# Attention in three products of float16 halves, with the order of projections, weight splits and turned outputs moved around it

## The chip, the cores and the metric

The kernel runs on one core of a Trainium2 chip. The metric is the time of one execution on the device in microseconds. A run of the program on the chip gives one such time; where a median is given, it is over several runs. A profile is one execution taken by the hardware profiler.

## What is computed

A decoder trunk of two layers on 256 tokens of width 1024, all in float32. Each layer normalises its input, projects it with one matrix into the inputs of four causal token mixers of four heads each (A: forgetting attention with a cumulative log-forget bias; B: sliding window with two key heads and sinks; C: multi-head latent attention with a rotary part; D: dilated windows), joins their outputs, projects them back and adds; then comes a feed-forward block, dense in layer 0, two of eight experts in layer 1. Cut to what matters here:

```python
for layer in range(DEPTH):                       # DEPTH = 2
    h = rms_norm(x, attn_norm[layer])
    (fq, fk, fv, ff, sq, sk, sv, cq, ckv, kr, dq, dk, dv) = jnp.split(h @ w_in[layer], splits, axis=-1)
    y_a, y_b, y_c, y_d = fox_mixer(...), swa_sink_mixer(...), mla_mixer(...), dilated_mixer(...)
    x = x + jnp.concatenate([y_a, y_b, y_c, y_d], axis=-1) @ w_out[layer]
    h = rms_norm(x, ffn_norm[layer])
    x = x + (swiglu(h, ...) if layer % 2 == 0 else moe_swiglu(h, ...))
return rms_norm(x, final_norm)
# in every mixer, a head: s = q @ k.T * scale + bias; p = softmax(s, causal); o = p @ v
```

## The kernel before

**Float16 halves of weights.** Every large weight is loaded as float32 by a DMA of about 1 MB that the SP queue issues (`load_next`, L162) and split on the chip into a high and a low float16 half: ScalarE writes the high one (`high_part`, L169), VectorE the low one, the rest (`low_part`, L172). A product with such a weight is three float16 matmuls (`mm3`, L458 to L461: high by high, high by low, low by high). `Stream` keeps the order: units of weights in the order of their use; `split_next` gives out one unit's high part and the low parts of the units before it; `done` counts a used unit and calls `go`, which splits up to `ahead` units past the used one (`ahead` starts at 3 and grows to 5, one at every second unit from the sixth on). `done` stops short of both while `later` is set.

**Attention in float32.** The projections leave q and k transposed (heads' columns in partitions) and v by tokens, as float32 tiles; `out_T` (L564) writes q and k from PSUM with one VectorE instruction that applies the scale and the norm factor `rb`. For head i of 16 (four each of A, C, D, B), `qk(i)` (L753) makes the scores of two blocks of 128 queries with float32 matmuls over 64 rows (C has a second product over 32 rows for its rotary part, A adds float16 products with a triangle, L774, for the forget bias), then VectorE adds the mask and takes the row extreme (L785) and ScalarE takes the exponential (L790). `tr(i)` (L799) transposes the probabilities on TensorE and copies them to `pT` on ScalarE (L805). `pv(i)` (L811) multiplies them with v in three float32 matmuls of 64 columns (L819); after a group's fourth head VectorE divides into `o` (L827), and `turn_out` (L833) transposes that and leaves the two halves of `mix` (L841, L842) for the output projection `wo_job`.

**Order.** Each engine runs its instructions in the order in which the program gives them out. The loop over i (L845 on) gives out, for each i: the scores of head i, a job of projection or of output projection from the queue `fills`, `pv` of head i - 2, `tr` of head i - 1. The fills are, in order: the two halves of D's q (the second with `mla_b`, which transposes the normalised latents), `mla_c` (the rotary q, q, k and v of C), `mla_d` with D's k, D's v, B's q, k and v, then the output projections of A, C, D. A's v, q and k come before the loop. `turn_out` of A, D and B stands ahead of the job of its turn, that of C behind it.

Of the kernel before, what the change touches and what calls it, by code (L numbers as in the profile page):

```python
# [11 lines left out]
F32 = mybir.dt.float32  # L12
F16 = mybir.dt.float16
# [26 lines left out]
C = 96  # L40
# [29 lines left out]
def hybrid_trunk_kernel(ctx: ExitStack, tc: tile.TileContext, a: dict, out: bass.AP, dbg=None):  # L70
# [56 lines left out]
    for layer in range(DEPTH):  # L127
# [9 lines left out]
        j = layer // 2  # L137
# [360 lines left out]
    def attention(layer, act, feed, follow):  # L498
# [11 lines left out]

        qT, kT, vv = {}, {}, {}

        def alloc(g):
            slot = "A" if g == "B" else g
            if g == "C":
                qT[g], kT[g] = (mid[:, c0 : c0 + 512].rearrange("p (j s) -> p j s", j=2) for c0 in (1024, 1536))
            else:
                qT[g] = act.tile([P, 2, S], F32, tag=f"q{slot}", name=f"q{g}_{layer}")
                kT[g] = act.tile([P, 2, S], F32, tag=f"k{slot}", name=f"k{g}_{layer}")
            vv[g] = act.tile([P, NT, 256], F32, tag=f"v{slot}", name=f"v{g}_{layer}")  # L520

        c_sb = late_t[:, : NT * 416].rearrange("p (t n) -> p t n", t=NT)
        psm = [bank("acc", f"mla{layer}{t}") for t in range(NT)]
# [37 lines left out]
                first_done.pop()()  # L561
            return ps

        def out_T(dst, ps, scale, p=(0, P), q=(0, P)):  # L564
            ve.scalar_tensor_tensor(
                dst[q[0] : q[1]], ps[p[0] : p[1], :S], scale, rb[p[0] : p[1], :], op0=OP.mult, op1=OP.mult
            )

        def job_T(g, d, m, scale):
            out_T(d[g][:, m, :], proj_T(m), scale)  # L570
            if m == 1:
                unit_done()

# [6 lines left out]

        def job_S(g, t, n, c0):
            ps = proj_S(t, n, c0)
            ve.tensor_scalar(vv[g][:, t, :n], ps[:, :n], rs[:, t : t + 1], None, op0=OP.mult)
            if t == 1:
                unit_done()

# [30 lines left out]
        late = {}  # L617

        def mla_b():
            cT = late_t[:, : 3 * S].rearrange("p (j s) -> p j s", j=3)  # L620
            late["cqT"], late["ckT"] = cT[:, 0:2], cT[:, 2]
            rT = late_t[:, 832:1600].rearrange("p (j s) -> p j s", j=3)
            late["qr"] = rT[:, 2].rearrange("p (t h i) -> p t h i", t=NT, h=4)
            late["qrT"], late["krT"] = rT[:, 0], rT[:, 1]
            p1, p2 = bank("acc", f"mt{layer}a"), bank("acc", f"mt{layer}b")
            for j in range(3):
                ps, c0 = (p1, j * S) if j < 2 else (p2, 0)
                for t in range(NT):
                    te.transpose(ps[:, c0 + t * P : c0 + (t + 1) * P], cn[:, t, j * P : (j + 1) * P], ident)
            for t in range(NT):  # L630
                te.transpose(p2[:, S + t * P : S + (t + 1) * P], kr[:, t, :, :].rearrange("p h i -> p (h i)"), ident)
            se.copy(late["cqT"], p1.rearrange("p (j s) -> p j s", j=2))
            ve.tensor_copy(late["ckT"], p2[:, :S])
            ve.tensor_copy(late["krT"], p2[:, S:])

        def mla_c():
            alloc("C")
            cqT, ckT = late["cqT"], late["ckT"]
            ps = bank("acc", f"mr{layer}")
            for t in range(NT):  # L640
                for k in range(2):
                    te.matmul(ps[:, t * P : (t + 1) * P], cqT[:, k, t * P : (t + 1) * P], wqr[:, k, :], start=k == 0, stop=k == 1)
            rope(ve, late["qr"], ps[:, :S].rearrange("p (t h i) -> p t h i", t=NT, h=4), 0, 4, rtmp)
            ps = bank("acc", f"mq{layer}")
            for j in range(2):
                for k in range(2):
                    te.matmul(ps[:, j * S : (j + 1) * S], wqn[:, k, j * P : (j + 1) * P], cqT[:, k, :], start=k == 0, stop=k == 1)
            se.activation(qT["C"], ps.rearrange("p (j s) -> p j s", j=2), AF.Copy, scale=-(96.0**-0.5))
            ps = bank("acc", f"mk{layer}")
            for j in range(2):  # L650
                te.matmul(ps[:, j * S : (j + 1) * S], wkn[:, j * P : (j + 1) * P], ckT, start=True, stop=True)
            se.copy(kT["C"], ps.rearrange("p (j s) -> p j s", j=2))
            ps = bank("acc", f"mv{layer}")
            for t in range(NT):
                te.matmul(ps[:, t * S : (t + 1) * S], ckT[:, t * P : (t + 1) * P], wkv, start=True, stop=True)
            se.copy(vv["C"], ps.rearrange("p (t s) -> p t s", t=NT))

        def mla_d():
            ps = bank("acc", f"mrt{layer}")
            for t in range(NT):  # L660
                te.transpose(ps[:, t * P : (t + 1) * P], late["qr"][:, t, :, :].rearrange("p h i -> p (h i)"), ident)
            se.copy(late["qrT"], ps[:, :S])

        QS = -(HD**-0.5)
        alloc("A")
# [1 line left out]
        for t in range(NT):  # L667
            ps = proj_S(t, 260)
            ve.scalar_tensor_tensor(z[:, t, :], ps[:, 256:260], rs[:, t : t + 1], bf_bc[:, layer, :], op0=OP.mult, op1=OP.add)
            ve.tensor_scalar(vv["A"][:, t, :], ps[:, 0:256], rs[:, t : t + 1], None, op0=OP.mult)  # L670
        unit_done()
        e1 = atile([P, NT, 4], "e1")
        ve.scalar_tensor_tensor(e1, z, -1.0, z, op0=OP.mult, op1=OP.min)
# [6 lines left out]
        ge.tensor_copy(lbh, lfb)  # L680
        ge.tensor_tensor(lbl, lfb, lbh, op=OP.subtract)
        for d, sc_ in ((qT, QS), (kT, 1.0)):
            stream[0].later = layer > 0 and d is qT
            for m in range(2):
                job_T("A", d, m, sc_)
                if m == 0 and d is qT:
                    mla_norm()
# [19 lines left out]
        def skjob():  # L707
            ps = proj_T(0)
            kb = kT["B"]
            out_T(kb[:, 0, :], ps, 1.0)  # L710
            out_T(kb[:, 1, :], ps, 1.0, (64, 128), (0, 64))
            out_T(kb[:, 1, :], ps, 1.0, (0, 64), (64, 128))

        def svjob():
            for t in range(NT):
# [37 lines left out]
        def qk(i):  # L753
# [1 line left out]
            ps = bank("sc", f"sc{layer}_{i}")  # L755
            b0 = 64 * (h % 2)
            m = h // 2
            q = qT[g][b0 : b0 + 64, m, :]
            k = kT[g][b0 : b0 + 64, (h % 2) ^ m if g == "B" else m, :]
            prods = [(q, k)]  # L760
            if g == "C":
                prods.append((late["qrT"][32 * h : 32 * h + 32, :], late["krT"][32 * h : 32 * h + 32, :]))
            for t in range(NT):
                nk = (t + 1) * P
                c0 = t * P
# [33 lines left out]
        def tr(i):  # L799
            tt = live[i]  # L800
            ps = bank("pt", f"tp{layer}_{i}")
            for j in range(3):
                te.transpose(ps[:, j * P : (j + 1) * P], tt[:, j * P : (j + 1) * P], ident)
            pT = act.tile([P, 384], F32, tag="pT", name=f"pT{layer}_{i}", bufs=2)
            se.copy(pT, ps[:, :384])  # L805
            live[i] = pT

        def pv(i):
            g, h = heads[i]
            pT = live.pop(i)  # L810
            if h == 0:  # L811
                live["o"] = bank("o", f"o{layer}_{i}")
            ps = live["o"]
            vh = h // 2 if g == "B" else h
            vc = slice(vh * 64, (vh + 1) * 64)
            for t in range(NT):
                for j in range(t + 1):
                    c0 = (t + j) * P
                    te.matmul(ps[:, t * S + h * 64 : t * S + (h + 1) * 64], pT[:, c0 : c0 + P], vv[g][:, j, vc], start=j == 0, stop=j == t)  # L819
# [23 lines left out]

        NHD = len(heads)
        for i in range(NHD + 3):  # L845
            if i < NHD:
                qk(i)
            if layer == 0 and i == 2:
                nc.sync.dma_start(bias[:, 1:], a["c_bias"][:, 1:])
            if layer == DEPTH - 1 and i in (5, 10, 16):  # L850
                stream[0].load_next({5: "e0", 10: "e2", 16: "e3"}[i])
            if i in (6, 14, 18):
                turn_out({6: "A", 14: "D", 18: "B"}[i])
            if i == NHD + 1 and layer == DEPTH - 1:
                late["gain"] = act.tile([P, 3, 384], F32, tag="tt", name="gain").rearrange("p a s -> p (a s)")[:, :D]
                ge.dma_start(late["gain"], spread(a["ffn_norm"][layer], D))
            if i == NHD:
                if layer < DEPTH - 1:
                    hold(True)
                else:  # L860
                    stream[0].low_until(stream[0].split)
            fills.popleft()()
            if i == 15:
                fills.popleft()()
            if i == 10:
                turn_out("C")
            if 0 <= i - 2 < NHD and i != 17:
                pv(i - 2)
            if 0 <= i - 1 < NHD:
# [533 lines left out]
```

## Time and profile before

| what | us |
|---|---|
| median of three runs (1367.72 to 1370.78) | 1368.82 |
| the profiled execution's own time | 1368.37 |
| its span, first to last instruction | 1366.6 |

The span runs through five stages: the start and A's projections, layer 0's attention, its dense block, layer 1's attention, the experts. [...] A timeline gives an instruction's (or a run of equal ones') start, its time, engine, line, operation, what it writes and reads, shape, count, and in brackets how long the engine had been idle and what ended that. Matmuls overlap their neighbours, so the step from one start to the next tells more than the time shown. A group of the costliest-groups view gives count, busy time, the mean time of one in ns, and the idle time before them.

### The profile page before, as it was taken

The numbers are of one execution on the slowest core, as the hardware profiler recorded it, in microseconds if no ns is written. First come the engines' busy times: TensorE is split into PE (matmuls) and PEld (weight loads), VectorE is DVE, ScalarE is ACT, GpSimd is POOL, SyncE is SP. The second block draws the span as 40 slices with busy tenths as digits, with TensorE's granted clock in tenths as the row PEclk, the third lists the DMA queues.
The fourth block names the chain that finished last, engine by engine and source line by source line (L and its number), as shares of the span: only waits on it lengthen the run. The fifth ranks groups of instructions, "written<-read, shape, count | busy, mean of one in ns | idle before, by whom it ended". The sixth has DMA issues, their size and how long they took to land.

```text
span 1366.6 us, 43224 instructions
## 1 busy us (share of the span) xinstructions
PE 1277.3 (93%) x19680; PEld 1134.5 (83%) x19680; DVE 1079.5 (79%) x1032; ACT 898.2 (66%) x916; POOL 32.4 (2%) x51
## 2 busy tenths in 40 slices
PE   8999999999999998999999998998998998999885
PEld 5785877777587688999989988998998998999874
DVE  6655775666564587899998898898898998989976
ACT  6554654444544576788777678677777776877764
POOL 2300000000010010000000000000000000000000
PEclk9999999999999999999999999999999999999998
DMA  9953475646443459999999999999999999999991
GB/s 272 353 171 124 155 247 198 203 149 203 156 172 111 175 196 392 400 406 414 413 411 416 412 412 416 411 411 412 408 414 402 403 416 408 410 405 407 412 361 57
DMA packets 128799, 434.35 MB, mean 318 GB/s; under 512 B 11936, under 2 KB 59440, under 8 KB 128480
## 3 DMA queue, kind: packets, MB, share of 16 engines
q1 hardware_dynamic: 126640, 429.72, 81.4%
q8 instruction: 156, 2.56, 0.8%
q0 software_dynamic: 928, 1.78, 0.5%
q14 instruction: 35, 0.29, 0.1%
q10 hardware_dynamic: 1040, 0.00, 0.0%
HBM read 430.41 MB, written 1.06 MB: 316 GB/s over the span
## 4 chain that ended last, share of the span: by engine, by line
PE 23%; DMA 19%; DVE 11%; issue 5%; ACT 3%; SPq 0%; DVEq 0%; ACTq 0%
DMA stg<-in_moe_w_down_dram 13%; DVE lo L172 8%; PE my L1190 5%; DMA stg<-in_moe_w_up_dram 3%; DMA stg<-in_moe_w_gate_dram 3%; PE mu L1151 2%; PE my L1192 2%; PE mg L1161 2%; PE mg L1158 2%; PE mg L1157 2%; PE mg L1151 1%; ACT hi L169 1%; PE mu L1158 1%; PE mu L1157 1%; PE mu L1161 1%
## 5 line engine op out<-in xcount | busy, mean ns | idle before, releaser
L172 DVE SCALAR_TENSOR_TENSOR lo<-stg,hi 128x1792 f16<-128x1792 f32 (+3 forms) x418 | 849.4, 2078 | 44.0 <-ACT hi L169 43.8
L169 ACT ACTIVATE hi<-stg 128x1792 f16<-128x1792 f32 (+3 forms) x418 | 714.4, 1738 | 154.0 <-DMA stg<-in_moe_w_down_dram 56.7
L1158 PEld LDWEIGHTS <-hi 128*128 128x128 f16 x3136 | 271.8, 98 | 11.3 <-issue 11.1
L1157 PEld LDWEIGHTS <-hi 128*128 128x128 f16 x3136 | 272.7, 99 | 4.2 <-issue 4.0
L1192 PE MATMUL my<-rest,hi 128*128 128x96 f16 x1792 | 182.9, 208 | 0.9 <-issue 0.9
L1190 PE MATMUL my<-rest,hi 128*128 128x96 f16 x1792 | 183.0, 208 | 0.3 <-issue 0.3
L1190 PEld LDWEIGHTS <-hi 128*128 128x128 f16 x1792 | 157.6, 99 | 6.2 <-issue 3.3
L1192 PEld LDWEIGHTS <-hi 128*128 128x128 f16 x1792 | 157.2, 99 | 4.1 <-issue 1.0
L1157 PE MATMUL mg<-xgh,hi 128*128 128x96 f16 x1568 | 151.3, 208 | 8.0 <-DVE x L1224 6.0
L1158 PE MATMUL mg<-xgl,hi 128*128 128x96 f16 x1568 | 151.5, 208 | 5.4 <-issue 5.3
L1161 PEld LDWEIGHTS <-lo 128*128 128x128 f16 x3136 | 146.3, 98 | 5.2 <-issue 3.5
L1157 PE MATMUL mu<-xgh,hi 128*128 128x96 f16 x1568 | 147.1, 206 | 0.1
L1158 PE MATMUL mu<-xgl,hi 128*128 128x96 f16 x1568 | 147.1, 206 | 0.0
L1190 PE MATMUL my<-rest,lo 128*128 128x96 f16 x1792 | 115.4, 208 | 7.9 <-DVE lo L172 7.2
L1190 PEld LDWEIGHTS <-lo 128*128 128x128 f16 x1792 | 89.6, 99 | 9.6 <-DVE lo L172 8.6
L1161 PE MATMUL mg<-xgh,lo 128*128 128x96 f16 x1568 | 86.7, 207 | 2.9 <-issue 2.9
L1161 PE MATMUL mu<-xgh,lo 128*128 128x96 f16 x1568 | 85.2, 206 | 0.1
L459 PEld LDWEIGHTS <-hi 128*128 128x128 f16 x640 | 62.6, 98 | 9.9 <-issue 2.7
L460 PEld LDWEIGHTS <-hi 128*128 128x128 f16 x640 | 62.6, 98 | 7.2
L461 PEld LDWEIGHTS <-lo 128*128 128x128 f16 x640 | 62.6, 98 | 7.2
L1179 ACT CAST rest<-sg 128x480 f16<-128x480 f32 (+1 forms) x48 | 27.1, 566 | 60.4 <-DVE sg L1178 60.4
L1151 PE MATMUL mu<-xr,stg 128*128 128x96 f32 x448 | 64.4, 312 | 0.0
(355 smaller groups left out, 1868.2 us busy)
## 6 DMA issues: line engine op xcount, KB each, us to landing
stg<-in_moe_w_gate_dram SPq DMA_DIRECT2D x128, 896.0 KB, 17.9
stg<-in_moe_w_up_dram SPq DMA_DIRECT2D x128, 896.0 KB, 17.4
stg<-in_moe_w_down_dram SPq DMA_DIRECT2D x111, 1024.0 KB, 19.2
stg<-in_w_in_dram SPq DMA_DIRECT2D x14, 1024.0 KB, 7.0
stg<-in_dense_w_gate_dram SPq DMA_DIRECT2D x14, 1024.0 KB, 6.5
stg<-in_dense_w_up_dram SPq DMA_DIRECT2D x14, 1024.0 KB, 5.1
stg<-in_dense_w_down_dram SPq DMA_DIRECT2D x14, 1024.0 KB, 5.0
stg<-in_w_out_dram SPq DMA_DIRECT2D x8, 1024.0 KB, 9.0
```

The source lines that it names most:

```text
L169: se.activation(self.high[u][:, c], self.stage[u][:, c], AF.Copy, scale=SW)
L172: ve.scalar_tensor_tensor(lo[:, c], self.stage[u][:, c], SW, self.high[u][:, c], op0=OP.mult, op1=OP.subtract)
L459: te.matmul(ps, lh, rh, start=first, stop=False)
L460: te.matmul(ps, lh, rl, start=False, stop=False)
L461: te.matmul(ps, ll, rh, start=False, stop=last)
L1151: te.matmul(ps[b][:, c * C : (c + 1) * C], w[0][:, j * P : (j + 1) * P], xr, start=False, stop=ends and j + 1 == spans[b][1])
L1157: te.matmul(dst, L, xh[:, k, :], start=k == 0 and c == 0, stop=False)
L1158: te.matmul(dst, L, xl[:, k, :], start=False, stop=False)
L1161: te.matmul(ps[b][:, c * C : (c + 1) * C], lo[:, j * P : (j + 1) * P], xh[:, k, :], start=False, stop=ends and j + 1 == spans[b][1])
L1179: se.copy(hi[:, c], sg[:, c])
L1190: te.matmul(dst, W, L[0], start=first and part == 0 and d % 4 == 0, stop=ends and part == 1 and d % 4 == 3)
L1192: te.matmul(dst, W, L[1], start=False, stop=False)
```

## The change

The q, k, v, the rotary parts and the transposed probabilities are kept as two float16 halves in the room of the float32 tile, and every product of the scores and of the values becomes three float16 products. The halves are made by `part2`: ScalarE copies the high one out of PSUM, VectorE subtracts. `out_T` first scales in place in PSUM, then calls `part2`; the second copy of B's keys, with the two heads' partitions exchanged, is made by two VectorE copies of the halves. Three changes of order go with it: at i = 0 the fill goes ahead of the scores of head 0; `later` is set for A's k in layer 0, for both q and k in layer 1, until the scores of head 1 are given out, and `go` is called there; `turn_out` of A and D goes behind the fill of its turn.

```diff
+        def part2(hi, lo, src, scale=None):
+            if scale is None:
+                se.copy(hi, src)
+                ve.tensor_tensor(lo, src, hi, op=OP.subtract)
+            else:
+                se.activation(hi, src, AF.Copy, scale=scale)
+                ve.scalar_tensor_tensor(lo, src, scale, hi, op0=OP.mult, op1=OP.subtract)
...
-        def out_T(dst, ps, scale, p=(0, P), q=(0, P)):
-            ve.scalar_tensor_tensor(
-                dst[q[0] : q[1]], ps[p[0] : p[1], :S], scale, rb[p[0] : p[1], :], op0=OP.mult, op1=OP.mult
-            )
+        def out_T(dst, ps, scale):
+            ve.scalar_tensor_tensor(ps[:, :S], ps[:, :S], scale, rb, op0=OP.mult, op1=OP.mult)
+            part2(dst[0], dst[1], ps[:, :S])
...
-            ve.tensor_scalar(vv[g][:, t, :n], ps[:, :n], rs[:, t : t + 1], None, op0=OP.mult)
+            part2(vv[g][:, 0, t, :n], vv[g][:, 1, t, :n], ps[:, :n], rs[:, t : t + 1])
...
-            ve.tensor_copy(late["krT"], p2[:, S:])
+            part2(late["krT"][:, 0], late["krT"][:, 1], p2[:, S:])
...
-            se.activation(qT["C"], ps.rearrange("p (j s) -> p j s", j=2), AF.Copy, scale=-(96.0**-0.5))
+            part2(qT["C"][:, 0], qT["C"][:, 1], ps.rearrange("p (j s) -> p j s", j=2), -(96.0**-0.5))
...
-            stream[0].later = layer > 0 and d is qT
+            stream[0].later = layer > 0 or d is kT
...
-            out_T(kb[:, 0, :], ps, 1.0)
-            out_T(kb[:, 1, :], ps, 1.0, (64, 128), (0, 64))
-            out_T(kb[:, 1, :], ps, 1.0, (0, 64), (64, 128))
+            out_T([kb[:, i, 0, :] for i in range(2)], ps, 1.0)
+            ve.tensor_copy(kb[0:64, :, 1, :], kb[64:128, :, 0, :])
+            ve.tensor_copy(kb[64:128, :, 1, :], kb[0:64, :, 0, :])
...
+            prods = [(qq[:, i], kk[:, j]) for qq, kk in pairs for i, j in ((0, 0), (0, 1), (1, 0))]
...
-            pT = act.tile([P, 384], F32, tag="pT", name=f"pT{layer}_{i}", bufs=2)
-            se.copy(pT, ps[:, :384])
+            pT = act.tile([P, 2, 384], F16, tag="pT", name=f"pT{layer}_{i}", bufs=2)
+            part2(pT[:, 0], pT[:, 1], ps[:, :384])
...
+                    mm3(ps[:, t * S + h * 64 : t * S + (h + 1) * 64], L, R, j == 0, j == t)
...
         for i in range(NHD + 3):
+            if i == 0:
+                fills.popleft()()
             if i < NHD:
                 qk(i)
+            if i == 1:
+                stream[0].later = False
+                stream[0].go()
...
-            if i in (6, 14, 18):
-                turn_out({6: "A", 14: "D", 18: "B"}[i])
...
-            fills.popleft()()
+            if i == 18:
+                turn_out("B")
+            if i > 0:
+                fills.popleft()()
             if i == 15:
                 fills.popleft()()
-            if i == 10:
-                turn_out("C")
+            if i in (6, 10, 14):
+                turn_out({6: "A", 10: "C", 14: "D"}[i])
```

## Rows read from the trace of the kernel before

**Rows 1.** The table by stages: stretch and length, then busy time and number of instructions of TensorE's matmuls, its weight loads, VectorE, ScalarE and GpSimd, the granted clock, the DMA share and GB/s. Layer 0's attention, the dense block, layer 1's attention, the experts.

```profile
43.00:137.00 94.00, 94.00 (x668) 68.82 (x669) 50.06 (x115) 46.27 (x108) 5.60 (x8) 1.00 0.61 205
137.00:359.00 222.00, 221.67 (x1746) 167.27 (x1745) 138.05 (x129) 99.78 (x91) 0.00 (x0) 1.00 0.58 193
387.00:480.00 93.00, 92.57 (x659) 67.88 (x660) 48.99 (x115) 44.27 (x105) 0.59 (x1) 1.00 0.40 136
...
497.00:1335.00 838.00, 777.55 (x15764) 761.63 (x15762) 757.23 (x502) 636.13 (x488) 0.61 (x1) 0.97 1.01 406
```

**Rows 2.** The timeline of TensorE's matmuls: a FoX head's scores between two projections, values and probabilities' transposes, an MLA head's scores, a dilated head's scores and the projection behind it, and 96-column float16 products of the experts.

```profile
47.20 0.48 PE L768 MATMUL sc<-kA,qA 64*128 64x128 f32 x2
47.62 0.28 PE L774 MATMUL sc<-cm,mid 128*128 128x128 f16 x2
47.84 0.70 PE L768 MATMUL sc<-kA,qA 64*128 64x256 f32 x2
48.47 0.50 PE L774 MATMUL sc<-cm,mid 128*128 128x256 f16 x4
48.80 0.27 PE L459 MATMUL pt<-hx_a,hi 128*128 128x256 f16 x1
...
64.21 0.78 PE L819 MATMUL o<-vA,pT 128*128 128x64 f32 x6
64.83 0.50 PE L803 MATMUL tp<-cm,tt 128*128 128x128 f32 x3
65.25 0.49 PE L768 MATMUL sc<-mid 64*128 64x128 f32 x2
...
67.34 0.28 PE L459 MATMUL pt<-hx_a,hi 128*128 128x256 f16 x1
...
93.29 0.92 PE L768 MATMUL sc<-kD,qD 64*128 64x128 f32 x4
94.14 0.28 PE L459 MATMUL pt<-hx_a,hi 128*128 128x256 f16 x1
94.26 0.27 PE L460 MATMUL pt<-hx_a,hi 128*128 128x256 f16 x1
...
667.66 0.21 PE L1190 MATMUL my<-rest,hi 128*128 128x96 f16 x1
...
667.96 0.21 PE L1192 MATMUL my<-rest,hi 128*128 128x96 f16 x1
```

**Rows 3.** Groups by line and shape over the whole span: what it does, count, busy us, mean ns of one, idle time before. Splits of weights, the copy of the probabilities, a 384-column and a 256-column read of PSUM on VectorE, weight loads on 64 and on 128 rows, a 512-column operation on VectorE.

```profile
L172 DVE SCALAR_TENSOR_TENSOR lo<-stg,hi 128x2048 f16<-128x2048 f32 x168 | 381.9, 2285 | 26.2 <-ACT hi L169 26.0
L169 ACT ACTIVATE hi<-stg 128x2048 f16<-128x2048 f32 x168 | 318.3, 1906 | 89.3 <-DMA stg<-in_moe_w_down_dram 56.0 <-PE fd L461 16.3 <-issue 6.7
L805 ACT COPY pT<-tp 128x384 f32<-128x384 f32 x32 | 15.3, 478 | 34.1 <-PE tp L803 33.9
L1087 DVE CAST xgl<-gx 128x384 f16<-128x384 f32 x16 | 8.8, 552 | 0.9 <-PE gx L1082 0.9
L819 PEld LDWEIGHTS o<-vD,pT 128*128 128x128 f32 x48 | 6.5, 192 | 0.9
L768 PEld LDWEIGHTS sc<-kD,qD 64*128 64x128 f32 x32 | 4.1, 186 | 1.3 <-issue 1.3
L827 DVE TENSOR_TENSOR o<-o,ll 128x512 f32<-128x512 f32 x8 | 5.5, 692 | 10.9 <-PE o L819 10.4
L565 DVE SCALAR_TENSOR_TENSOR kD<-pt,late 128x256 f32<-128x256 f32 x4 | 1.7, 424 | 8.1 <-PE pt L461 8.1
```

**Rows 4.** Timelines of layer 0's start: VectorE, then TensorE; last a 256-column copy out of PSUM on ScalarE, some jobs later.

```profile
39.89 0.41 DVE L565 SCALAR_TENSOR_TENSOR qA<-pt,late 128x256 f32<-128x256 f32 x1
40.23 2.27 DVE L172 SCALAR_TENSOR_TENSOR lo<-stg,hi 128x2048 f16<-128x2048 f32 x1
...
42.89 0.49 PE L768 MATMUL sc<-kA,qA 64*128 64x128 f32 x2 [1.78 <-DVE kA L565]
...
62.91 0.35 ACT L662 COPY late<-mrt 128x256 f32<-128x256 f32 x1
```

**Rows 5.** Timelines of layer 1's start: ScalarE, TensorE.

```profile
384.33 3.69 ACT L169 ACTIVATE hi<-stg 128x2048 f16<-128x2048 f32 x2
...
387.43 0.49 PE L768 MATMUL sc<-kA,qA 64*128 64x128 f32 x2 [1.27 <-DVE kA L565]
...
398.86 1.11 PE L642 MATMUL mr<-early,late 128*128 128x128 f32 x8
```

**Rows 6.** Timelines around a pair of splits in layer 0's attention: VectorE, ScalarE, TensorE.

```profile
70.51 4.48 DVE L172 SCALAR_TENSOR_TENSOR lo<-stg,hi 128x2048 f16<-128x2048 f32 x2
...
72.38 0.46 ACT L805 COPY pT<-tp 128x384 f32<-128x384 f32 x1
...
75.72 0.78 PE L819 MATMUL o<-vA,pT 128*128 128x64 f32 x6
```

**Rows 7.** The table by stages (columns as in rows 1) at two places where TensorE was little used.

```profile
487.00:490.00 3.00, 1.19 (x9) 0.39 (x7) 2.45 (x13) 2.27 (x4) 0.00 (x0) 1.00 0.01 3
490.00:493.00 3.00, 2.05 (x21) 1.60 (x21) 2.69 (x5) 1.35 (x3) 0.00 (x0) 0.52 0.00 0
...
529.00:532.00 3.00, 0.19 (x5) 0.09 (x3) 2.18 (x4) 0.73 (x2) 0.00 (x0) 1.00 1.02 418
...
535.00:538.00 3.00, 2.58 (x33) 2.58 (x33) 2.29 (x2) 0.10 (x1) 0.34 (x1) 0.50 1.02 408
```

More of the change, by code (lines that the diff above doesn't have):

```diff
@@ L511, in attention, with halves @@
         qT, kT, vv = {}, {}, {}
+        def halves(room, j):
+            return room.bitcast(F16).rearrange("p (i j s) -> p i j s", i=2, j=j)
+        def part2(hi, lo, src, scale=None):
[5 more added lines that the diff above has]
+                ve.scalar_tensor_tensor(lo, src, scale, hi, op0=OP.mult, op1=OP.subtract)
         def alloc(g):
@@ L515, in alloc @@
             if g == "C":
-                qT[g], kT[g] = (mid[:, c0 : c0 + 512].rearrange("p (j s) -> p j s", j=2) for c0 in (1024, 1536))
+                qT[g], kT[g] = (halves(mid[:, c0 : c0 + 512], 2) for c0 in (1024, 1536))
             else:
-                qT[g] = act.tile([P, 2, S], F32, tag=f"q{slot}", name=f"q{g}_{layer}")
-                kT[g] = act.tile([P, 2, S], F32, tag=f"k{slot}", name=f"k{g}_{layer}")
-            vv[g] = act.tile([P, NT, 256], F32, tag=f"v{slot}", name=f"v{g}_{layer}")
+                qT[g] = act.tile([P, 2, 2, S], F16, tag=f"q{slot}", name=f"q{g}_{layer}")
+                kT[g] = act.tile([P, 2, 2, S], F16, tag=f"k{slot}", name=f"k{g}_{layer}")
+            vv[g] = act.tile([P, 2, NT, 256], F16, tag=f"v{slot}", name=f"v{g}_{layer}")
         c_sb = late_t[:, : NT * 416].rearrange("p (t n) -> p t n", t=NT)
@@ L562, in proj_T @@
             return ps
-        def out_T(dst, ps, scale, p=(0, P), q=(0, P)):
-            ve.scalar_tensor_tensor(
-                dst[q[0] : q[1]], ps[p[0] : p[1], :S], scale, rb[p[0] : p[1], :], op0=OP.mult, op1=OP.mult
-            )
+        def out_T(dst, ps, scale):
+            ve.scalar_tensor_tensor(ps[:, :S], ps[:, :S], scale, rb, op0=OP.mult, op1=OP.mult)
+            part2(dst[0], dst[1], ps[:, :S])
         def job_T(g, d, m, scale):
-            out_T(d[g][:, m, :], proj_T(m), scale)
+            out_T([d[g][:, i, m, :] for i in range(2)], proj_T(m), scale)
             if m == 1:
@@ L623, in mla_b @@
             late["qr"] = rT[:, 2].rearrange("p (t h i) -> p t h i", t=NT, h=4)
-            late["qrT"], late["krT"] = rT[:, 0], rT[:, 1]
+            late["qrT"], late["krT"] = (halves(rT[:, i], 1)[:, :, 0, :] for i in range(2))
             p1, p2 = bank("acc", f"mt{layer}a"), bank("acc", f"mt{layer}b")
@@ L651, in mla_c @@
                 te.matmul(ps[:, j * S : (j + 1) * S], wkn[:, j * P : (j + 1) * P], ckT, start=True, stop=True)
-            se.copy(kT["C"], ps.rearrange("p (j s) -> p j s", j=2))
+            part2(kT["C"][:, 0], kT["C"][:, 1], ps.rearrange("p (j s) -> p j s", j=2))
             ps = bank("acc", f"mv{layer}")
@@ L655, in mla_c @@
                 te.matmul(ps[:, t * S : (t + 1) * S], ckT[:, t * P : (t + 1) * P], wkv, start=True, stop=True)
-            se.copy(vv["C"], ps.rearrange("p (t s) -> p t s", t=NT))
+            part2(vv["C"][:, 0], vv["C"][:, 1], ps.rearrange("p (t s) -> p t s", t=NT))
         def mla_d():
@@ L661, in mla_d @@
                 te.transpose(ps[:, t * P : (t + 1) * P], late["qr"][:, t, :, :].rearrange("p h i -> p (h i)"), ident)
-            se.copy(late["qrT"], ps[:, :S])
+            part2(late["qrT"][:, 0], late["qrT"][:, 1], ps[:, :S])
         QS = -(HD**-0.5)
@@ L669, in attention @@
             ve.scalar_tensor_tensor(z[:, t, :], ps[:, 256:260], rs[:, t : t + 1], bf_bc[:, layer, :], op0=OP.mult, op1=OP.add)
-            ve.tensor_scalar(vv["A"][:, t, :], ps[:, 0:256], rs[:, t : t + 1], None, op0=OP.mult)
+            part2(vv["A"][:, 0, t, :], vv["A"][:, 1, t, :], ps[:, 0:256], rs[:, t : t + 1])
         unit_done()
@@ L757, in qk @@
             m = h // 2
-            q = qT[g][b0 : b0 + 64, m, :]
-            k = kT[g][b0 : b0 + 64, (h % 2) ^ m if g == "B" else m, :]
-            prods = [(q, k)]
+            q = qT[g][b0 : b0 + 64, :, m, :]
+            k = kT[g][b0 : b0 + 64, :, (h % 2) ^ m if g == "B" else m, :]
+            pairs = [(q, k)]
             if g == "C":
-                prods.append((late["qrT"][32 * h : 32 * h + 32, :], late["krT"][32 * h : 32 * h + 32, :]))
+                pairs.append((late["qrT"][32 * h : 32 * h + 32], late["krT"][32 * h : 32 * h + 32]))
+            prods = [(qq[:, i], kk[:, j]) for qq, kk in pairs for i, j in ((0, 0), (0, 1), (1, 0))]
             for t in range(NT):
@@ L818, in pv @@
                     c0 = (t + j) * P
-                    te.matmul(ps[:, t * S + h * 64 : t * S + (h + 1) * 64], pT[:, c0 : c0 + P], vv[g][:, j, vc], start=j == 0, stop=j == t)
+                    L, R = ((z[:, 0, c], z[:, 1, c]) if r is None else (z[:, 0, r, c], z[:, 1, r, c]) for z, r, c in (
+                        (pT, None, slice(c0, c0 + P)), (vv[g], j, vc)))
+                    mm3(ps[:, t * S + h * 64 : t * S + (h + 1) * 64], L, R, j == 0, j == t)
             if h == 3:
```

## The prediction

> **What bounds the kernel now.** I read the table by stages first [rows 1]. In layer 0's attention (43 to 137 us) TensorE is busy 94.0 of 94 us, VectorE 50.1 and ScalarE 46.3; the dense layer (137 to 359) is 221.7 of 222 us of TensorE, with DMA at 0.58; layer 1's attention (387 to 480) is 92.6 of 93. From 497 to 1335 the DMA share is 1.01 at 406 GB/s: the experts are bound by weight traffic. What is saved in layer 0 therefore comes straight through the dense layer, and what is saved in layer 1 lets the stream of expert weights restart earlier, whose length the change does not touch. So every microsecond of TensorE time before 480 us counts once, unless another engine then ends last. The timeline of TensorE [rows 2] gives the prices of its products, the groups by shape [rows 3] those of ScalarE and VectorE, and the timelines of the two starts [rows 4, 5] and of one burst of weight splits [rows 6] tell how much room there is for the other engines to be late.
>
> **Scores.** Each f32 product is two instructions that stream their columns twice. The set of a FoX head takes 0.42 us for 128 keys (47.20 to 47.62) and 0.63 for 256 (47.84 to 48.47) [rows 2]; 0.21 and 0.43 of that is streaming, the rest (0.21) is a weight load in the open plus a drain of some 0.1 us whenever the rows used change from 64 to 128: two 128-column products at 47.62 need 0.11 but the next set starts 0.22 later, while the four products at 48.47 (two of 256 columns, two of 128) and the 128-row one at 48.80 follow each other without a gap, 0.33 us in all [rows 2]. That is 0.11 us for a float16 product of 256 columns and 0.055 for one of 128. A set of three is then 0.17 or 0.33, plus the drain and a first load of some 0.02 (after a drain, 94.14 to 94.26 is 0.12 for 0.11 of streaming): 0.28 and 0.45. A FoX head saves 0.14 + 0.18 = 0.32 us. An MLA head has two such sets per block of queries (65.25 to 67.34, 2.09 us): 0.64. A dilated or window head, both blocks in one run (0.85 us, 93.29 to 94.14), becomes 0.62: 0.23. No row shows a float16 load on 64 rows. Its bounds are 0.02 (128-row float16) and 0.11 in the open before every product (the first f32 load above); f32 loads take the same time on 64 rows (186 ns) as on 128 (192) [rows 3], so I take the float16 128-row end and keep the other as a rival. Per layer: 4 x 0.32 + 4 x 0.64 + 8 x 0.23 = 5.7 us.
>
> **Values.** Three f32 products of 64 columns take 0.62 us (64.21 to 64.83), the pace of their loads [rows 2]. Nine float16 products replace them. The nearest row is the experts' 96-column stream, each product with its own 128-column load, 0.042 us apart (667.66 to 667.96, seven steps) [rows 2]; 64 columns lie between 0.028 (two thirds of it) and 0.042. I take 0.03: 0.27 us, saving 0.35 a head, 5.6 us a layer (0.24 and 3.8 at the other end). [...]
>
> **TensorE's total:** 11.3 us a layer. The transposes of probabilities stay f32.
>
> **What VectorE and ScalarE get.** A low half of the probabilities is 16 subtractions of 384 columns at 0.55 us (the nearest row, a 384-column read of PSUM, 552 ns [rows 3]) = 8.8 us a layer. Eleven halves of q and k at 0.42 [rows 3] are 4.6, MLA's three 512-column halves 2.1 (0.69 each [rows 3]), the rest about 0.5: 16 us for VectorE, which goes from 50 to 66 of some 90. ScalarE gets eleven copies of 0.35 [rows 4] and v's six of 0.4: about 6 us. Neither is full. But out_T, one 0.42 us instruction until now, becomes a chain over two in-order engines, 0.42 + 0.35 + 0.42, and VectorE stands still behind the middle link: 1.2 us before its next out_T can start. And pT reaches the value products through the copy (0.48) and the subtraction (0.55), each behind whatever weight split is queued there: 1.90 us on ScalarE, 2.28 on VectorE [rows 3].
>
> **Start, layer 0** [rows 4]. Now the first score waits 1.78 us for kA, whose out_T stands behind a split (40.23, 2.27 us). That split is the low half of the weights of DQ, which the projection that is now moved ahead multiplies by; VectorE begins it only after qA's second out_T (39.89). After the change out_T takes 0.9 longer, and v's halves, now on ScalarE in front of a split, delay the chain by 0.3: the low half is there at about 43.7. TensorE, done with kA at 41.0, does two products and waits 2.6 us; the projection ends at 46.1, kA's halves about then, and the score goes without more wait. The old wait of 1.8 goes, one of 2.6 comes. mla_a's rotations on GpSimd go ahead of the score too; nothing waits for them before the transposes of mla_b.
>
> **Splits one head later.** They stand behind two softmaxes and ahead of mla_b's copies: on ScalarE the split of the deferred unit, DQ's second copy and one more split come before the copy cqT, without which mla_c's first product can't start. In layer 0 one unit is deferred (the allowance no longer grows at that step); I walk cqT to 55.0 and TensorE to 53.7: a wait of 1.3 us. In layer 1 two units are deferred, and their high halves, which ran at 384.33 while ScalarE was idle [rows 5], come after the second softmax (394.6): 396.5, 398.4, then DQ's copy at 399.2 behind two low halves, one more split, cqT at 402.1. TensorE gets there at 398.4: 3.7 us (it started at 398.86 before). Layer 1's first score also waits: qA's second out_T starts at 386.9 there, then two of kA's at 1.2 each, 390.6, against a projection that ends at 388.6: 2.0 us in place of 1.27 [rows 5]. The deferred splits also put back the refills on SP's queue by a head, some 4 us; the units are used five jobs on and DMA stands at 0.4 to 0.6 in attention [rows 1], which hides it. If it did not, a transfer or two late would cost about a split, 2 us.
>
> **Bursts in the middle.** In layer 0, DK's end lets two splits go, VectorE 70.51 to 74.99; pT(3), copied at 72.38 by ScalarE, was in time for its products at 75.72 [rows 6]. Now pT(3) needs a subtraction behind that burst and TensorE is faster: 1.6 us of wait. Since the allowance grows a step later, SQ's end has such a pair too, beside a dilated head whose TensorE time is only 0.27 + 0.43 + 0.62 + 2.62 = 3.9 us: 2.4. In layer 1 the closes bring one split each: none. svjob's pair of out-copies and a split: 1.0 in each layer. The output turned one job later gives o, now later on VectorE, a job's cover, but D's mix then has only one head (1.4 us) before wo reads it: 0.2. At the end the layer's last split stands ahead of the last two pT: 2.0.
>
> **Sum.** Layer 0: -11.3 - 1.8 + (2.6 + 1.3 + 1.6 + 2.4 + 1.0 + 0.2 + 2.0 = 11.1) = -2.0. Layer 1: -11.3 - 1.3 + (2.0 + 3.7 + 1.0 + 0.2 + 2.0 = 8.9) = -3.7. The profiled execution took 1368.4 (span 1366.6), 0.4 under the median of 1368.8: 1368.4 - 5.7 = 1362.7.
>
> **Rivals.** (1) Clean pipeline: the middle and end waits (5.2 + 2.0 and 3.2) don't come since TensorE's own waits give VectorE time; 5.7 + 10.4 = 16: 1352. For it: no wait in the middle of attention now, ScalarE and VectorE half idle [rows 1]. [...] (3) Slower, VectorE's backlog in every head: from a job's end, out_T to its subtraction (1.4), a split (2.3) and pT's subtraction (0.5) make 4.2, TensorE's round 3.9; if handing over costs more than 0.1 to 0.2 a link, all closes of units, not three, hold the value products, some 1.2 us at five more places in each layer, and 1.0 more at the first score: 14 us less 3 that overlap: 1374. It decides from the point where that chain passes the round. (4) Float16 loads on 64 rows in the open: 120 products a layer, 0.09 each, 11 us, of which half falls into waits: 1374. f32 speaks against it: four 64-row instructions in 0.85 us, of which 0.64 is streaming and 0.1 the drain [rows 2], leave room for one open load. [...]
>
> **Chances.** Forecast 0.42 (own range 1358 to 1367), clean 0.18, clock 0.17, backlog 0.18, loads 0.05. 0.2% (2.7 us, about what a measurement of this kernel tells from none) lies at 1366.1: faster 0.36 + 0.18 + 0.07 = 0.61; same 0.06 + 0.08 + 0.02 = 0.16; slower 0.23. The range runs from the clean case to just short of the backlog: 1352 to 1372.
>
> **What would show it.** Right: value products of a head in 0.27 to 0.4 us, score sets of 0.28 and 0.45; waits of TensorE at DQ's third product, at mr (more in layer 1), at pT(3) and pT(7). Wrong: score sets no shorter than now; no wait over 0.5 us after mla_c (clean), or one in every head (backlog); a granted clock under 0.9 at 400 to 410 (clock). It would be most wrong if a refill came late enough to hold the dense layer.

## The result and the profile after

| kernel | median, us | runs | against before, 95% interval |
|---|---|---|---|
| before | 1368.83 | 1367.72 to 1370.78 | |
| after | 1380.59 | 1379.22 to 1382.16 | 1.0085 [1.0067, 1.0102] |

The changed kernel is 0.85% slower, where 1362.7 was forecast. Its profiled execution took 1382.2 us, the longest of its four, with a span of 1380.4. The table by stages of the kernel after, the first three stretches and the columns of [rows 1], and behind them short stretches of layer 0's attention:

```profile
43.00:137.00 94.00, 81.43 (x713) 57.03 (x714) 62.31 (x140) 50.41 (x117) 5.62 (x8) 0.95 0.59 197
137.00:359.00 222.00, 221.67 (x1748) 167.41 (x1746) 138.81 (x130) 101.12 (x93) 0.00 (x0) 1.00 0.59 195
387.00:480.00 93.00, 83.89 (x728) 61.41 (x726) 61.06 (x148) 49.65 (x124) 4.83 (x9) 0.92 0.39 130
...
86.00:88.00 2.00, 0.00 (x0) 0.00 (x0) 1.96 (x2) 0.92 (x2) 0.00 (x0) 1.00 0.00 0
88.00:90.00 2.00, 1.98 (x16) 1.16 (x17) 0.56 (x1) 0.48 (x1) 0.00 (x0) 0.98 0.70 216
90.00:92.00 2.00, 2.00 (x10) 1.35 (x10) 0.64 (x4) 0.99 (x4) 0.00 (x0) 0.50 0.90 308
```

TensorE, busy in nearly all of both attentions before, now stands still 12.6 of 94 us in layer 0 and 9.1 of 93 in layer 1, and its granted clock, as a share of full speed 1.00 in both before, is 0.95 and 0.92. The dense layer is as it was, and from the turned output of B in layer 1 to the end it is 892.6 us, 893.0 before. So the loss is made ahead of that, in the two attentions and at their starts, by waits and by the clock. The list of waits of TensorE, 30 to 500 us (us in total, times, longest):

```profile
PE tp L816 <- DVE mix L857: 9.4, 4, 3.2
PE o L461 <- DVE pT L521: 6.5, 8, 1.1
PE pt L461 <- DVE lo L172: 3.8, 1, 3.8
PE mr L654 <- ACT late L644: 2.9, 2, 2.1
PE o L459 <- ACT pT L520: 1.1, 2, 1.0
PE sc L781 <- ACT kA L520: 1.0, 1, 1.0
```

The lines below the first are the waits that the prediction speaks of. The first is in no list of mine: the transposes of a head's probabilities (`tr`, L816) wait for VectorE's subtraction of a *turned output* (`turn_out`, L857). Timelines of layer 0 show why: TensorE, then VectorE, then ScalarE.

```profile
78.30 0.34 PE L781 MATMUL sc<-mid 64*128 64x128 f16 x3
78.57 0.34 PE L781 MATMUL sc<-late 32*128 32x128 f16 x3
78.84 0.50 PE L781 MATMUL sc<-mid 64*128 64x256 f16 x3
79.27 0.50 PE L781 MATMUL sc<-late 32*128 32x256 f16 x3
79.70 0.40 PE L459 MATMUL pv<-hi,hx_a 128*128 128x256 f16 x1
...
83.97 0.60 PE L853 MATMUL ot0A<-cm,o 128*128 128x128 f32 x4
84.41 0.19 PE L459 MATMUL o<-vC,pT 128*128 128x64 f16 x1
...
84.64 0.19 PE L461 MATMUL o<-vC,pT 128*128 128x64 f16 x1
88.02 0.55 PE L816 MATMUL tp<-cm,tt 128*128 128x128 f32 x3 [3.19 <-DVE mix L857]
...
89.90 0.39 PE L459 MATMUL pt<-hx_a,hi 128*128 128x256 f16 x1
90.09 0.42 PE L460 MATMUL pt<-hx_a,hi 128*128 128x256 f16 x1
...
105.23 0.67 PE L781 MATMUL sc<-kD,qD 64*128 64x128 f16 x6
105.83 0.23 PE L459 MATMUL pv<-hi,hx_a 128*128 128x128 f16 x1
...
85.08 2.28 DVE L172 SCALAR_TENSOR_TENSOR lo<-stg,hi 128x2048 f16<-128x2048 f32 x1
87.28 0.68 DVE L857 TENSOR_TENSOR mix<-ot0A,mix 128x512 f16<-128x512 f32 x1
...
84.55 1.90 ACT L169 ACTIVATE hi<-stg 128x2048 f16<-128x2048 f32 x1
86.35 0.58 ACT L856 CAST mix<-ot0A 128x512 f16<-128x512 f32 x1
```

`turn_out` of A and D takes its PSUM tile from the group "pt", which is one single bank of the kernel's eight, and so does `tr`. Before, the job of 2.6 us lay between the two, and `tr` had no wait:

```profile
78.85 0.65 PE L838 MATMUL ot0A<-cm,o 128*128 128x128 f32 x4
79.34 0.27 PE L459 MATMUL pv<-hi,hx_a 128*128 128x256 f16 x1
...
81.96 0.78 PE L819 MATMUL o<-vC,pT 128*128 128x64 f32 x6
82.58 0.50 PE L803 MATMUL tp<-cm,tt 128*128 128x128 f32 x3
```

Now only value products of 0.26 us lie there. The bank is free when ScalarE has copied the turned output (86.35, behind a split's high half) and VectorE has subtracted (87.28, behind a low half); `tr` starts at 88.02, 3.19 us late. And at 90.09 the projection's products stand 0.21 us apart instead of 0.11 [rows 2], at a granted clock of 0.50, after TensorE had stood still from 84.8 to 88.0; from 88 to 90, right behind the wait, it was still 0.98.

### The profile page after: what moved, and what is told of

The parts are those of the page before. It is cut to its first block, busy times and chain, and to the rows that moved or that the text cites. A ratio compares the mean times of both kernels' runs of the same rounds, so it can differ in the third digit from the quotient of the medians.

```text
span 1380.4 us, 43666 instructions
## 1 busy us (share of the span) xinstructions
PE 1268.3 (92%) x19856; PEld 1118.9 (81%) x19856; DVE 1105.9 (80%) x1094; ACT 908.2 (66%) x952; POOL 32.6 (2%) x51
## 4 chain that ended last, share of the span: by engine, by line
DMA 30%; PE 15%; DVE 8%; issue 4%; ACT 2%; DVEq 0%; SPq 0%; ACTq 0%
DMA stg<-in_moe_w_down_dram 14%; DMA stg<-in_moe_w_up_dram 8%; DMA stg<-in_moe_w_gate_dram 8%; DVE lo L172 6%; PE my L1211 3%; PE my L1213 2%; PE mu L1172 1%; PE mg L1178 1%; ACT hi L169 1%; PE mg L1182 1%; PE mg L1179 1%; PE mu L1182 1%; PE mu L1179 1%; PE mu L1178 1%; PE mg L1172 1%
## 5 line engine op out<-in xcount | busy, mean ns | idle before, releaser
L1179 PEld LDWEIGHTS <-hi 128*128 128x128 f16 x3136 | 271.5, 98 | 13.3 <-issue 13.2
L461 PE MATMUL dg<-hx_f,lo 128*128 128x256 f16 (+1 forms) x240 | 62.5, 265 | 0.0
```

Of the source, the lines that this page charges most:

```text
L461: te.matmul(ps, ll, rh, start=False, stop=last)
L1179: te.matmul(dst, L, xl[:, k, :], start=False, stop=False)
```

## The experiments

**T1:** the one bank that `turn_out` and `tr` share is the cause. **T2:** part of the loss is the clock that falls after a wait. **T3**, the rival (the prediction's own slower case): VectorE is behind in every head, so that waits removed in one place come back in another.

In what was expected of e1 to e4, e11 and e12, T1 and T3 have this sense. In e5 to e7 and from e9 on, those two apart, T1 stands for order (short work that TensorE waits for is queued behind a weight split) and T3 for VectorE's whole load.

The change in pieces. The edits, shortened, on the kernel after (e1, e2, e3) and on that before (e4, e11, e12):

```diff
# e1, the turned outputs of A and D ahead of the job, as before
+            if i in (6, 14, 18): turn_out({6: "A", 14: "D", 18: "B"}[i])   # ahead of fills
-            if i == 18: turn_out("B")
-            if i in (6, 10, 14): turn_out({6: "A", 10: "C", 14: "D"}[i])   # behind
+            if i == 10: turn_out("C")
# e2, A in a bank of the projections, where C has it
-            ps = bank("acc" if g == "C" else "pt", f"ot{layer}{g}")
+            ps = bank("acc" if g in "AC" else "pt", f"ot{layer}{g}")
# e3 = e1 and, undone: fills.popleft()() ahead of qk(0); stream[0].later for kA, go() at i == 1
# e4 = before (f32) with all three changes of order; e11 = with the two that e3 undoes
# e12 = before (f32) with the turned outputs of A and D behind the job alone
```

> The changed kernel, with the outputs of A and D turned ahead of the job, where the kernel before has them. T1 (one PSUM bank): the transposes of a turned output and those of the head's probabilities use the same single bank; with no job between them TensorE waits until ScalarE and VectorE have read the output (3.19 and 1.63 us in layer 0, 3.19 and 1.42 in layer 1, 9.4 in all) and then runs at half clock for some microseconds. The waits should go, with 2 to 6 us of half clock: 1365 to 1370 us. T3 (backlog): VectorE is behind in every head, the bank is only where the backlog shows; the waits move to the value products, and the time stays within 3 us of the changed kernel's 1380.6.

> The changed kernel with its order, but A's output is turned in one of the four banks of the projections; D's stays in the bank of the probabilities (at that point the output projection holds all four). T1: the two waits of 3.19 us go with the half clock behind them, D's 1.63 and 1.42 stay: 1369 to 1374 us. If it is the order of the jobs by itself, not the bank: no change from 1380.6.

> Only the float16 halves, with the whole order of the kernel before: the first score ahead of the projection, the splits at the end of kA, the outputs ahead of the job. T1: no bank wait; what the halves cost VectorE and ScalarE shows at the first score and in a few value products, 1358 to 1366 us. T3: the halves themselves make the backlog: 1374 us or more.

> Only the three changes of order, with the f32 products of the kernel before. T1: the bank wait stands in f32 as well, some 2 to 3 us for A and 1 to 2 for D in each layer, and the half clock behind it: 1374 to 1381 us. T3: without the halves VectorE has no backlog, the order costs nothing: 1367 to 1371 us.

> The f32 kernel of before with two of the changes of order: a projection ahead of the first score and the splits one head later. T1 (the bank makes the loss): at most 3 us of loss, 1367 to 1372 us. T3: most of e4's 12.3 us of loss is here, 1376 us or more.

> The f32 kernel of before with the third change of order alone: the outputs of A and D turned behind the job. T1: TensorE waits for the bank at the transposes behind each, 2 to 3 us for A and 1 to 2 for D in each layer, with half clock behind it, and nothing else changes: 1375 to 1381 us. T3: 1367 to 1371 us.

| run | median | against before, 95% interval |
|---|---|---|
| e1 | 1371.6 | 1.0018 [1.0009, 1.0027] |
| e2 | 1370.5 | 1.0013 [1.0005, 1.0022] |
| e3 | 1370.2 | 1.0011 [1.0002, 1.0020] |
| e4 | 1381.3 | 1.0090 [1.0077, 1.0103] |
| e11 | 1368.4 | 1.0003 [0.9994, 1.0012] |
| e12 | 1381.1 | 1.0096 [1.0081, 1.0111] |

This settles the sign. The late turned output alone, in f32, without one float16 half, loses 12.6 us against the 1368.4 of e11, which has the other two changes of order and loses nothing that can be measured. Taking it back (e1) or giving A another bank (e2) brings 9 to 10 us, where the change loses 11.8; e1 ends 1.6 us above the range that T1 gave it. By T3 e12 would have lost nothing. e12, waits and TensorE's timeline in layer 0:

```profile
PE tp L803 <- DVE mix L842: 6.3, 4, 2.3
```

```profile
81.29 0.78 PE L819 MATMUL o<-vC,pT 128*128 128x64 f32 x6
84.39 0.55 PE L803 MATMUL tp<-cm,tt 128*128 128x128 f32 x3 [2.32 <-DVE mix L842]
...
86.84 1.22 PE L768 MATMUL sc<-late 32*128 32x256 f32 x2
87.99 0.39 PE L459 MATMUL pt<-hx_a,hi 128*128 128x256 f16 x1
88.17 0.42 PE L460 MATMUL pt<-hx_a,hi 128*128 128x256 f16 x1
```

The waits are 6.3 us, half of the loss. The clock accounts for the other half, 0.50 from 88 to 91 us, where it was 1.00 before: from `tr` behind A's output to the next value products it takes 8.4 us in each layer, and 5.1 before. In layer 0 a 256-column set takes 1.15 us (86.84 to 87.99) where it took 0.63 [rows 2], and the projection behind it 4.8 (87.99 to 92.82) where it took 2.6 (24 products 0.11 apart). Behind D's waits of 0.8 us the clock stayed at 1.00.

e3 missed its expectation, and that is the second finding: the halves alone, in the order of before, gain nothing. Its waits of TensorE in layer 0 (30 to 140 us):

```profile
PE sc L781 <- ACT kA L520: 4.6, 1, 4.6
PE o L461 <- DVE pT L521: 3.3, 4, 1.1
```

With the smaller ones they are 10.3 us here and 8.1 in layer 1, against 1.8 and 1.3 of before [rows 4, 5]: 15.3 more. The granted clock is 0.95 from 30 to 140 and from 375 to 500, where it was 1.00 and 0.97: up to 5.5 + 2.5 = 8 us. Together they take up all of the 22.6 that the forecast had TensorE save.

The clock by itself. e8 keeps the bank wait of the changed kernel and gives TensorE something to do in it:

```diff
+            live["sc"] = ps              # in qk
...
             if i in (6, 10, 14):
                 turn_out({6: "A", 10: "C", 14: "D"}[i])
+                if i != 10:   # unused columns of the score bank
+                    keep_warm({6: 40, 14: 16}[i], live["sc"][:, 384:512], ident16, tri16[:, :P])
```

> The changed kernel, and in the two waits for the bank (behind A's and D's turned outputs) TensorE does 40 and 16 float16 products of 128 columns into unused columns of the score bank, 2.2 and 0.9 us of work at full clock. T2 (the clock falls after a wait and the next jobs run at half speed): the waits stay, the jobs behind them return to 2.7 and 1.5 us from 4.5, 4.0 and 2.7: 4 to 6 us less, 1374 to 1377 us. If the long jobs behind the waits have another cause: 1380 us or more.

Measured: 1378.8, 1.0080 [1.0067, 1.0093]. Timeline of TensorE in e8, and the table by stages:

```profile
86.84 2.40 PE L322 MATMUL sc<-cm 128*128 128x128 f16 x40
...
90.28 0.55 PE L817 MATMUL tp<-cm,tt 128*128 128x128 f32 x3 [0.78 <-DVE mix L858]
...
92.16 0.28 PE L459 MATMUL pt<-hx_a,hi 128*128 128x256 f16 x1
```

```profile
92.00:94.00 2.00, 2.00 (x20) 1.66 (x18) 0.64 (x4) 0.98 (x4) 0.00 (x0) 1.00 1.05 363
```

The bank comes free no earlier (`tr` starts 4.1 us after A's output in both kernels), but the projection behind it now takes 2.6 us (92.16 to 94.79) at full clock instead of 4.3 (89.90 to 94.19); the same in layer 1. T2 is shown at these places. The median is 1.8 us under that of the kernel after, less than T2 expected, and the two intervals overlap, so that a gain of the whole is not shown. In this execution the first score started 1.1 us later, and the half clock ahead of A's output was longer (the projection from 81.09 took 5.1 us, 4.3 in the kernel after).

Then the question was where the halves' saving goes, and whether it can be had. e5 to e7, one upon the other from e3 on (in e5 the layer's last split also goes behind the last value products, in e6 the splits of kA's close behind the first projection):

```diff
# e5: a closed unit gives out no split; the splits follow the transposed probabilities
+            if not self.behind: self.go()
...
                 tr(i - 1)
+            if i < NHD: stream[0].go()
# e6: e5, and MLA's normalisation behind kA; A and D turned in the bank of the value sums
-                if m == 0 and d is qT: mla_norm()
+        mla_norm()                       # behind the loop over qA and kA
+            ps = bank({"A": "o", "C": "acc", "D": "o", "B": "pt"}[g], f"ot{layer}{g}")
# e7: e6 with f32 products
```

> The float16 halves with the order of before (as e3), but the weight splits that a closed unit lets go are given out behind the head's transposed probabilities, not ahead of them, and the last split of the layer behind the last value products. T1 (the low half of the probabilities waits on VectorE behind a split): the waits at the value products of heads 3, 8, 14 and 15 (1.28, 0.77, 0.36 and 1.07 us in layer 0 of e3) and part of the half clock behind them go: 1362 to 1367 us. T3 (VectorE is behind by its whole load, not by its order): the waits move, 1369 to 1372 us.

> e5, and MLA's normalisation given out behind the halves of kA instead of between the two blocks of qA, the splits of kA's close behind the first projection, and the outputs of A and D turned in the bank of the value sums instead of that of the probabilities. T1: the first score waits 0.8 to 1.3 us instead of 4.57 and 3.57 (e3), the waits of 0.6 to 0.8 at the turned outputs go, and the half clock that follows these waits: 8 to 15 us under e5, 1350 to 1358 us. T3: VectorE's added 16 us a layer have to go somewhere, 1365 us or more.

> The order of e6 with the f32 products of the kernel before: no halves. It tells what the order gains by itself. T1: the first score's waits (1.78 and 1.27 us before) shrink to nothing and little else changes: 1364 to 1367 us, so that e6 against e7 is the halves' own gain, 7 to 15 us. T3: e6 is no faster than e7.

Measured: e5 1371.0 (1.0017 [1.0008, 1.0025]), e6 1366.5 (0.9987 [0.9979, 0.9996]), e7 1364.4 (0.9971 [0.9961, 0.9981]). e5 and e6 missed as T3 says: the waits moved. In e6's layer 0 they stand here:

```profile
PE mr L655 <- ACT late L645: 2.9, 1, 2.9
PE ot0A L854 <- DVE o L843: 2.5, 1, 2.5
PE o L460 <- ACT pT L521: 1.9, 1, 1.9
```

Each has a pair of splits, or a single one, on VectorE and ScalarE ahead of it. So it was not yet decided whether VectorE has too much to do or only has it in bursts. e9 to e18 tell this apart (`one` gives out a single split if one is due):

```diff
# e9: e6 with at most one split a head, from head 1 to 14; e10: e9 in f32
-            if i < NHD: stream[0].go()
+            if 1 <= i < 15: stream[0].one()
# e13: e9, A turned behind the job in a bank of "acc", splits from head 1 to 12
# e15: e13 with splits from head 1 to 13
# e17: e15 and one split behind the last score; e18: e17 in f32
                 qk(i)
+            if i == 15: stream[0].one()
# e14, e16: e9 and e15 with a projection ahead of the first score
```

> e6 with at most one weight split a head, given out behind that head's transposed probabilities, none beside the first score and none between heads 15 and the end. T1 (bursts of two splits hold softmax, MLA's copies and the turned output on VectorE and ScalarE: in e6 2.86 us before mr, 2.55 before A's turned output, 1.92 before head 14's products, each with half clock behind it): these go, 8 to 18 us under e6, 1349 to 1359 us. T3 (VectorE's load is the limit): the waits spread over the heads, 1364 us or more.

> The order of e9 with f32 products. T1: f32 has hardly a wait left in e7 (0.33 us in layer 0), so one split a head gains nothing: 1363 to 1366 us, and e9 against e10 is what the float16 halves are worth where the other engines are given their place. T3: e9 is no faster than e10.

> e9 without the waits that are left in it: A's output is turned behind the job in a bank of the projections (in e9 0.99 us for the output and 1.81 for its bank), and the last split comes with head 12, so that none stands ahead of the output of D and the probabilities of head 14 (0.58 and 1.92). T1: 3 to 5 us in layer 0 and 2 to 4 in layer 1 with the half clock behind these waits: 1352 to 1356 us. T3 (VectorE's load): the waits move elsewhere, 1359 us or more.

> e9 with the change's projection ahead of the first score. In e9 the first score waits 0.17 and 0.25 us for kA in layer 0 and not at all in layer 1, so there is nothing to cover; the projection's products with the low half of DQ's weights could come early: 1360 to 1363 us, no gain. If it covers something that the trace does not show: 1358 us or less.

> e13 with head 13's split given out again (none at head 14 and behind). If the dense layer's 3.82 us of waiting in e13 is the missing split: it goes, with the half clock behind it, 1350 to 1354 us. If the dense layer has another limit: 1356 us as e13.

> e15 with the change's projection ahead of the first score. Where the first score waits less than 0.5 us there is nothing to cover: within 2 us of e15. If its products wait for DQ's low half or its jobs lie in the way of kA's halves: 2 us or more above e15.

> e15 with one more split, behind the softmax of the last head, where neither the probabilities of head 14 nor those of head 15 stand behind it for long. If this is the split that the dense layer waits for: its 3.82 us and the half clock behind it go, 1350 to 1353 us. If not: 1357 us as e15, or more if the split holds the last value products.

> e17's order with the f32 products of the kernel before. If the gain of e17 is the halves': 1363 to 1366 us, as e10 (whose TensorE has no wait left to lose), so that the halves are worth 10 to 13 us of the 22.6 that they save in TensorE's work. If it is the order's: 1358 us or less.

| run | products | median | against before, 95% interval |
|---|---|---|---|
| e9 | float16 | 1360.2 | 0.9944 [0.9928, 0.9961] |
| e10 | f32 | 1364.9 | 0.9973 [0.9964, 0.9982] |
| e13 | float16 | 1356.5 | 0.9912 [0.9898, 0.9925] |
| e14 | float16 | 1356.5 | 0.9908 [0.9892, 0.9923] |
| e15 | float16 | 1357.0 | 0.9919 [0.9905, 0.9932] |
| e16 | float16 | 1356.4 | 0.9915 [0.9901, 0.9928] |
| e17 | float16 | 1353.0 | 0.9884 [0.9868, 0.9901] |
| e18 | f32 | 1366.3 | 0.9989 [0.9980, 0.9998] |

One split a head was worth 6 us with halves, less than the 8 to 18 that T1 gave it, and nothing in f32 (e7 and e10 are alike). e13's attention was shorter still, but its dense layer waited, on TensorE's timeline:

```profile
145.68 0.40 PE L466 MATMUL du<-hx_f,lo 128*128 128x256 f16 x1 [3.82 <-DVE lo L172]
```

e15 gave head 13 its split back and missed: the wait stayed at 3.82 us. e17 put one behind the last score, and it was gone. e17 beats both kernels, by 15.4 us the one before. Its layer 0 attention, dense layer and layer 1 attention in the table by stages, and the wait of TensorE that is longest in total (30 to 480 us):

```profile
40.80:121.90 81.10, 77.01 (x712) 55.20 (x712) 61.41 (x147) 50.18 (x125) 6.47 (x12) 0.98 0.70 235
127.50:352.90 225.40, 225.07 (x1767) 169.52 (x1766) 139.27 (x133) 102.10 (x99) 0.00 (x0) 1.00 0.58 190
379.40:459.60 80.20, 76.84 (x714) 55.18 (x714) 58.77 (x145) 48.27 (x124) 1.18 (x3) 0.98 0.41 140
```

```profile
PE o L464 <- ACT pT L525: 2.8, 2, 1.5
```

VectorE is busy 61.4 of 81.1 us, with about the work that it has in the kernel after (59.4 of 88.6 us between the same two points). T3's load is not the limit; the queue of splits ahead of short work that TensorE needs is real, and order removes most of its waits. e18 against e17 is the halves alone: 1366.3 - 1353.0 = 13.3 us (14.4 by the two ratios) of the 22.6 forecast. From the first score to B's turned output e18 takes 86.9 and 86.7 us, e17 81.1 and 80.2. The rest, 9.3 us, is waits and clock: all waits of e17's two attentions make 7.7 us, those of e18 1.3, and a clock of 0.98 over 161 us up to 3.2.

Whether a projection ahead of the first score gives anything stays open. Beside e15, on the same chip, e16 shows no difference. e14 lies below e9, but these two ran at different times, and both spread over 7 us (e9 1356.45 to 1363.13, e14 1355.17 to 1362.82).

## Why the prediction was wrong, by its steps

**The step that failed** is the one on the turned output: it "gives o ... a job's cover", and D's mix costs 0.2. I followed the data (value sums to output, output to projection) and not the bank. The 9.4 us of `tr` behind `mix`, and the half clock behind most of them, are in no term of the sum and in no rival. The job that was moved away was also the cover of the bank; the question "what is late if that cover is gone" was asked of it for o alone.

**The clock** had a chance of 0.17 and one sign, under 0.9 from 400 to 410 us. The sign came (0.83), but the clock fell behind waits all over both attentions: (1 - 0.95) x 94 + (1 - 0.92) x 93 = 12.1 us at most, by the first table. At that bound it is larger than the bank's 9.4. A part of it hangs on the bank: from `tr` behind A's output to the next value products it takes 6.2 and 7.0 us in the two layers, and 4.5 in e8 at full clock. Not every wait had it: behind D's 1.63 us in layer 0 the clock stayed at 1.00 (128 to 132 us).

**The sum again.** Forecast 1362.7; the bank +9.4; the waits that I did list, 20.0 forecast, measured 3.8 + 6.5 + 2.9 + 1.1 + 1.0 + 0.4 (two small ones) = 15.7: -4.3; the clock up to +12.1. That gives at most 1379.9; the execution that these waits are read from took 1382.2, the median is 1380.6. Some 2 us of it stay open.

**What held.** Score sets: 0.27 and 0.43 us for an MLA head (78.30 to 78.57, 78.84 to 79.27; forecast 0.28 and 0.45), 0.60 for a dilated head (105.23 to 105.83; 0.62). At 0.055 and 0.11 us a product [rows 2], each leaves 0.10 over, at the change of the rows in use, and the dilated head's six products on the same rows leave it once. The f32 sets take 0.42 and 0.63 us [rows 2]: 0.21 for 128 more columns, near four times the 0.055 of a float16 product. The drain and the loads by which the forecast accounts for the rest, here and there, are its estimate; how it divides is not shown. Value products: eight steps in 0.23 us (84.41 to 84.64), 0.26 for a head (0.27). VectorE: from 50 to 62 us in the stretch of layer 0 (16 forecast; the stretch now ends with B's turned output, before it reached 8 us further). The saving of TensorE was nearly there. It can be read where the clock stayed at 1.00: in layer 1 of e13, from the first score to B's output, TensorE is busy 75.4 us, and 86.2 before, 10.8 less (11.3 forecast):

```profile
383.50:460.90 77.40, 75.35 (x713) 54.66 (x713) 55.59 (x144) 46.77 (x123) 1.11 (x3) 1.00 0.41 134
```

Of the waits, DQ's third product was 3.75 us (2.6), mr 0.80 and 2.14 (1.3 and 3.7), the values of head 3 1.3 (1.6), of head 7 2.1 (2.4), the end 1.4 (2.0): the right places, each off by 0.3 to 1.6 us.

A weight load of these value products takes 0.10 us in the trace, as long as three or four of the steps of 0.029 at which nine products with a load each start: the loads overlap. The six products of a 64-row set take 0.50 of their 0.60 us by the prices above, which leaves no room for six loads of 0.10 us in the open.

**The rivals.** The clean pipeline is not what this order gives; e17 shows that 1353.0, almost its number, can be had with another order, though not as a clean pipeline: 7.7 us of waits are left in it. The backlog in every head would have been 1374 and had the right sign, but not the reason: the low half held the value products 8 times in 32 heads, and e12 has no halves and loses as much. Loads on 64 rows are refuted by the score sets.

With one bank for both, `tr` waited 3.19 us behind A's output in each layer; with another for A (e2) these two waits are gone, and D's two, 3.0 us in all, are left.

## What to carry to other kernels

When an operation is moved past another, list not only who reads its result but who next needs each room it holds, its PSUM bank above all: two operations that share one bank are coupled, and what lies between them is a cover (a job of 2.6 us left no wait here, value products of 0.26 left 3.19). Splitting an operand for cheaper products turns one read-out (0.48 us for the probabilities) into a chain over two engines (0.48 and 0.56), each of which can stand behind a weight split (of 1.90 and 2.28 us, as the two reads of A's output at 86.35 and 87.28); give the short links out ahead of the long work in those queues, and the long work one piece at a time, or the saving comes back as waits (10.3 and 8.1 us in e3's two layers, 1.8 and 1.3 before). Price a wait of TensorE by itself and by the jobs behind it, which may run at half clock (4.3 us for a job of 2.6, behind A's wait in layer 0).

## What the runs showed of the hardware that was not expected

The same wait may cost the clock or not. In e9 and e14, TensorE waits 1.81 us for the same bank, behind the same projection and ahead of the same scores. Timelines of e9, then of e14:

```profile
79.73 0.19 PE L464 MATMUL o<-vC,pT 128*128 128x64 f16 x1 [1.81 <-DVE mix L862]
...
81.41 0.50 PE L786 MATMUL sc<-late 32*128 32x256 f16 x3
81.84 0.28 PE L464 MATMUL pt<-hx_a,hi 128*128 128x256 f16 x1
```

```profile
80.40 0.19 PE L464 MATMUL o<-vC,pT 128*128 128x64 f16 x1 [1.81 <-DVE mix L862]
...
82.71 0.82 PE L786 MATMUL sc<-late 32*128 32x256 f16 x3
83.46 0.39 PE L464 MATMUL pt<-hx_a,hi 128*128 128x256 f16 x1
```

In e9 the scores take 0.43 us and the clock stays at 1.00; in e14 they take 0.75, and the clock is 0.50 from 83 to 86. From the wait's end to the next head's first score it makes 5.5 us (85.2) against 8.6 (89.0). That fits the spread of 7 us over the runs of e9 and e14, where e10, without such waits, spreads over 2. What decides it was not found; the wait just ahead, for A's output, was the longer one in e9 (0.99 us, 0.34 in e14).
